# Hybrid gated-conv and forgetting-attention layer on one core: score buffers 192 bytes apart, later column sums, a residual added on TensorE, root and reciprocal in the final norm

## The chip, the cores and the metric

One Trainium2 chip, one core. The metric is the device time of the kernel in microseconds; three runs of the kernel before gave 702.77, 702.11 and 702.26 us, median 702.26 us. One further execution, of 702.7 us, was taken with the hardware profiler; its span (first to last instruction of the program) is 700.7 us. All rows of the profile and the trace are from that execution.

The engines go by short names: PE is TensorE (matmuls), PEld its loading of weights, DVE is VectorE, ACT is ScalarE, POOL is GpSimd, SP is SyncE (which only issues DMAs here). "L304" is line 304 of the kernel.

## The reference

One layer, 512 tokens of 1024 features, all in float32:

```
h = rms_norm(x) * g                       # over 1024 features
[cb|cc|cin|q|k|v|f|gates] = h @ w_in
y_conv = (cb * causal_dwconv3(cc * cin)) @ w_out_conv
F = cumsum(log_sigmoid(f))
o = softmax(q.k / 8 + F[t] - F[s], s <= t) v          # 8 heads of 64
m = sigmoid(g_A) * y_conv + sigmoid(g_B) * (o @ w_out_attn)
x = x + m @ w_o
h = rms_norm(x) * g_ffn
[a|b] = causal_dwconv3(h @ w_up)                      # 2 x 2816
x = x + (silu(a) * b) @ w_down
out = rms_norm(x) * g_final
```

`rms_norm(x)` is x / sqrt(mean(x^2) + 1e-6).

## The kernel before

**Data layout.** Features lie on the 128 partitions, in eight blocks of 128 (`KB`), tokens along the free axis (512). The residual stream is `x1`, called x in the trace. A matmul multiplies a weight tile of 128 x 128 by 256 tokens.

**Precision.** A float32 product is made of three matmuls on rounded halves: each operand is split into a high part (`h`) and the rest (`l`), and wh.xh, wl.xh and wh.xl are summed in PSUM (`mm3`, L286; `passes`, L304). The weights arrive raw in chunks, in the order of a list `stream`. For each chunk, `split` writes the high part with an ACT copy (L255, wh) and the rest with a DVE subtraction (L259, wl).

**Stages.** V projection; q and k projections with the attention scores between them; gates and the merge; w_o; the up projection with convolution and Silu (L1042), in two phases; the down projection, also in two phases, by a scheme of seven products for blocks of two by two (`seven`), with the additions collected in `combine`; at the end the last two feature blocks of the down projection as plain products (`plain7`, tiles pdA and pdB), and the final norm.

**Scores.** `scores` makes one 128-query tile of q.k for one head: a matmul of a_q (weights) with a_k (moving, L575), and a correction with qb (weights) and kb (moving, L576), into the same PSUM bank, 32 times in all. The moving width is 256, 384 or 512. These tiles come from a pool `ap`, which gives addresses in the order of allocation.

**Deferred work.** `later` holds small operations, each with the chunk number from which it is due, its estimated time and the PSUM banks that it frees. `run_later` pops due ones behind a split, `flush(banks)` pops from the front until no entry is left that touches those banks (all of them, without banks). The squares and the final scaling of the first six feature blocks (`final_square`) go through this list; the first two of them carry a due number, the others are due at once. On ACT a square is an activation from x (L1123, L1126), followed by a scaling of x (L1128), and on DVE an addition into ssq (L1127).

**The end.** `kall` is the list of the ten k-steps of a plain block. The tokens are in two halves: A (0 to 255) and B. The order on PE is written out by hand: both plain blocks of half A; five k-steps of the first block of half B (pdB6); the column sums of half A; the other five; the broadcast of half A's norm; the second block of half B (pdB7) in full; three filler matmuls (`warm_on`); the column sums of half B; six fillers; the broadcast of half B.

- `fin_sum` adds the residual (DVE, L1193), squares (ACT, L1195) and scales (ACT, L1196).
- `fin_col` adds one square into ssq (DVE, L1201) and calls `rstd_col`: the sums over the partitions (pc_n, L319, four passes for ssq and four for the last square), the mean plus eps (ms_n, DVE, L324) and the power -0.5 (rc_n, POOL, L326).
- `fin_out` broadcasts the result over the partitions with two matmuls (pb_n, L333), copies it for POOL (rs, ACT, L1208), multiplies (L1212) and sends the output.

Of the kernel before, what the change touches and what calls it, by code (L numbers as in the profile page):

```python
# [8 lines left out]
F32 = mybir.dt.float32  # L9
F32R = mybir.dt.float32r  # L10
AF = mybir.ActivationFunctionType
ALU = mybir.AluOpType

P = 128
D = 1024
S = 512
KB = D // P
NT = S // P
H = 8
# [3 lines left out]
NP = FFN // P  # L23
EPS = 1e-6
# [4 lines left out]
NPP = 4  # L29
# [5 lines left out]
G1, G2, GF, BG, CM, CF, BF = 0, 8, 16, 24, 40, 52, 184  # L35
# [31 lines left out]
def block_kernel(ctx, tc, xT, vecs, wv, win, wmix, wo, wup, wst, wdp, outT):  # L67
# [3 lines left out]
    nc = tc.nc  # L71
    PSUM = bass.MemoryType.PSUM

    cp = ctx.enter_context(tc.tile_pool(name="cp", bufs=1))
# [3 lines left out]
    def keep(ins):  # L78
        return tc.keep_in_program_order(ins)

    def bank(i, name):
        return ps.tile([P, S], F32, tag=f"b{i}", name=name)
# [14 lines left out]
    def col(i):  # L97
        return vec[:, i : i + 1]

    ident = cp.tile([P, P], F32, tag="ident", name="ident")  # L100
# [4 lines left out]
    tbl = cp.tile([4 * H, 1], F32, tag="tbl", name="tbl")  # L105
# [17 lines left out]
    n = 0  # L123
# [21 lines left out]
    raws, parts, order = [], [], {}  # L145
    pools = {"raw": wp}
    later = []
    held = dict.fromkeys(NRAW, 0)

    def after_split():  # L150

        st = ExitStack()
        for ins in order.values():
            st.enter_context(tc.issue_after(ins))
        return st
# [70 lines left out]

    def flush(banks=None):

        while any(banks is None or set(w[2]) & set(banks) for w in later):
            with after_split():  # L230
                later.pop(0)[3]()

    def split(hl=None):

# [72 lines left out]
            ))  # L307
            seen.add(bk)

    ex = cp.tile([P, NT], F32, tag="ex", name="ex")  # L310
    nc.gpsimd.memset(ex, -0.5)

    def rstd_col(sums, n, bc, name):


        pc = bank(bc, f"pc_{name}")
        for i, sq in enumerate(sums):
            for t in range(n):
                keep(nc.tensor.matmul(  # L319
                    pc[:, t : t + 1], sq[:, t * P : (t + 1) * P], ones[:, 0:1],  # L320
                    start=i == 0 and t == 0, stop=i == len(sums) - 1 and t == n - 1,
                ))
        ms = cp.tile([P, NT], F32, tag="ms", name=f"ms_{name}", bufs=2)
        nc.vector.tensor_scalar(ms[:, :n], pc[:, :n], 1.0 / D, EPS, op0=ALU.mult, op1=ALU.add)  # L324
        rc = cp.tile([P, NT], F32, tag="rc", name=f"rc_{name}", bufs=2)
        nc.gpsimd.tensor_tensor(rc[:, :n], ms[:, :n], ex[:, :n], op=ALU.pow)  # L326
        return rc
# [28 lines left out]
    ap = at.enter_context(tc.tile_pool(name="ap", bufs=1, side="right"))  # L356

    def ct(name):
        return ap.tile([P, S], F32, tag="ct", name=name, bufs=NCT)
# [15 lines left out]

    v2 = ap.tile([P, NT, 4, 2, 2, HD], F32R, tag="v2", name="v2")

    ssq = ct("ssq1")
    pa = [bank(t, f"pa{t}") for t in range(NT)]
    pb_ = [bank(4 + t, f"pb{t}") for t in range(NT // 2)]  # L380
# [3 lines left out]
    def load_x(kb, cs=slice(0, S)):  # L384
        if kb == len(xs):
            if kb % 2 == 0:
                load_x.t = ap.tile([P, 2, S], F32, tag="qt" if kb < 4 else "ka", name=f"xs{kb}", bufs=2)
            xs.append(load_x.t[:, kb % 2, :])
        keep(nc.sync.dma_start(xs[kb][:, cs], xT[:, kb, cs]))


    halves = [slice(0, S // 2), slice(S // 2, S)]
    load_x(0, halves[0])
    load(0)
    load_x(0, halves[1])
    for kb in range(1, AHEAD + 1):
        load_x(kb)
# [15 lines left out]
    for kb in range(KB):  # L413
        x = xs[kb]
# [70 lines left out]

    QB = [ap.tile([P, 2, S], F32R, tag=f"qb{i}", name=f"qb{i}") for i in range(2)]
    KBt = [ap.tile([P, 2, S], F32R, tag=f"kb{i}", name=f"kb{i}") for i in range(2)]
    AUX = (HD, 0)  # L490
    for t in (*QB, *KBt):
        tf = t.bitcast(F32)
# [8 lines left out]
    def evac_qk(pr, isq):  # L501
        def f(p):
# [6 lines left out]
            a = ap.tile([P, 2, S], F32R, tag="qt" if isq else "ka", name=f"a_{nm}", bufs=2)  # L509
            b = (QB if isq else KBt)[pr % 2]  # L510
            (QT if isq else KA)[pr] = a
# [58 lines left out]
    def scores(pr, e, qb):  # L570
# [5 lines left out]
        keep(nc.tensor.matmul(  # L576
            s[:, :nn], QB[pr % 2][: KR[e], e, qs], KBt[pr % 2][: KR[e], e, :nn], start=False, stop=True
        ))
# [72 lines left out]
    n = 4 * H  # L651
# [62 lines left out]
    for idx in late:  # L714
        kind, i = divmod(idx, 4)
# [7 lines left out]
    n = len(units)  # L723
    make_forms(0, len(GATES), "gate")
    for i in range(n + LA):
# [8 lines left out]
        if 0 <= i - LA < n:  # L734
            pr, e, qb = units[i - LA]
# [95 lines left out]
    def x_sums(qs):  # L831
        b11, b12, b21, b22 = (xq[:, qs, i, :] for i in range(4))

        def f():
            nc.vector.tensor_sub(b11, b11, b12)
            nc.vector.tensor_sub(b12, b22, b12)

        def g():
            nc.vector.scalar_tensor_tensor(b22, b11, -1.0, b22, op0=ALU.mult, op1=ALU.subtract)
            nc.vector.scalar_tensor_tensor(b21, b22, -1.0, b21, op0=ALU.mult, op1=ALU.subtract)  # L840

        return f, g
# [9 lines left out]
    for q in (0, 2):  # L852
        f, g = x_sums(slice(q, q + 2))
# [56 lines left out]
    for j in range(KB):  # L910
# [20 lines left out]
        a, b = gs  # L931
# [6 lines left out]
    x1 = xp.tile([P, KB, S], F32, tag="x1", name="x1")  # L938
# [70 lines left out]
    fp = ctx.enter_context(tc.tile_pool(name="fp", bufs=1))  # L1009
# [13 lines left out]
    def place(ph, q):  # L1023
        return (q - PHASES[ph][0] // 2) * (NF + ph)
# [13 lines left out]
    def glu(ph, j, uu):  # L1038
        a, b = uu
        q, k = j // 2, len(parts) - 1  # L1040
        g0 = place(ph, q)
        nc.scalar.activation(a, a, AF.Silu)  # L1042
        if j % 2 == 0:
            ge = glu.even = fp.tile([P, 2, 2 * P], F32, tag="ge", name=f"ge{q}", bufs=2)
            keep(nc.gpsimd.tensor_mul(ge, a.rearrange(halves_of, h=2), b.rearrange(halves_of, h=2)))  # L1045
            return
        flush()
        ge = glu.even
        go = fp.tile([P, 6, 2 * P], F32, tag="gr", name=f"go{q}")

        def mul(eng):
            return eng.tensor_mul(go[:, 0:2, :], a.rearrange(halves_of, h=2), b.rearrange(halves_of, h=2))

        if j + 1 < PHASES[ph][1]:
            keep(mul(nc.gpsimd))
        else:
            later.append((k + 3, 0.7, (("q", q),), lambda: mul(nc.vector)))
        b11, b12 = ge[:, 0, :], ge[:, 1, :]
        b21, b22, t1, t2, t3, t4 = (go[:, i, :] for i in range(6))

        def t13():
            nc.vector.tensor_sub(t1, b11, b12)
            nc.vector.tensor_sub(t3, b22, b12)

        def t24():
            nc.vector.scalar_tensor_tensor(t2, t1, -1.0, b22, op0=ALU.mult, op1=ALU.subtract)
            nc.vector.scalar_tensor_tensor(t4, t2, -1.0, b21, op0=ALU.mult, op1=ALU.subtract)

        def hl(src, gs):
            def f():  # L1070
                nc.scalar.activation(gh[:, gs, :], src, AF.Copy)
                nc.vector.tensor_sub(gl[:, gs, :], src, gh.bitcast(F32)[:, gs, :])

            return f


        d = (2, 3, 4) if j + 1 < PHASES[ph][1] else (4, 5, 6)
        w = [(d[0], 0.85, t13), (d[0], 0.85, t24), (d[1], 0.7, hl(ge[:, : 1 + ph, :], slice(g0, g0 + 1 + NF * ph, NF)))]
        w += [(d[x > 0 and 2 or 1], 0.7, hl(go[:, x : x + 2, :], slice(g0 + 1 + x, g0 + 3 + x))) for x in (0, 4, 2)]
        for n, us, f in w:  # L1080
            later.append((k + n, us, (("q", q),), f))
# [88 lines left out]
    kall = range(*PHASES[1])  # L1170

    def plain(m, t, ks, p, opens, closes):
        for k in ks:
            wh, wl = where[m, k]
            g = place(1, k // 2) + SLOT[k % 2][t]
            mm3(p, wh, wl, gh[:, g, :], gl[:, g, :], opens and k == kall[0], closes and k == kall[-1])

    m6 = KB - 2
# [6 lines left out]
    pd = ((pdA[:, th[0]], pdA[:, th[1]]), (pdB6[:, th[0]], pdB7[:, th[0]]))  # L1185

    def plain7(m, t, ks):
        plain(m6 + m, t, ks, pd[t][m], m == 0 or t == 1, m == 1 or t == 1)

    def fin_sum(t, m):  # L1190

        y = x1[:, m6 + m, halves[t]]
        nc.vector.tensor_add(y, pd[t][m], y)  # L1193
        sq = fp.tile([P, S], F32, tag="fu", name=f"sq3_{m}{t}", bufs=3)[:, : S // 2]
        nc.scalar.activation(sq, y, AF.Square)  # L1195
        nc.scalar.activation(y, y, AF.Copy, scale=col(GF + m6 + m))  # L1196
        return sq

    def fin_col(t, sqs):
        s_ = ssq3[:, halves[t]]  # L1200
        nc.vector.tensor_add(s_, s_, sqs[0])  # L1201
        return rstd_col([s_, sqs[1]], 2, 3 + t, f"n3{t}")

    def fin_out(t, rc):
        hs = halves[t]
# [15 lines left out]
    for m in range(2):  # L1221
        plain7(m, 0, kall)
    sqA = [fin_sum(0, 0), fin_sum(0, 1)]
    plain7(0, 1, kall[:5])
    rcA = fin_col(0, sqA)
    plain7(0, 1, kall[5:])
    fin_out(0, rcA)
    sqB = [fin_sum(1, 0)]
    plain7(1, 1, kall)
    sqB.append(fin_sum(1, 1))  # L1230
    warm_on(3)
    rcB = fin_col(1, sqB)
# [100 lines left out]
```

## Time and the profile before

| what | value |
|---|---|
| median of three runs | 702.26 us (702.11 to 702.77) |
| profiled execution | 702.7 us, span 700.7 us |
| granted TensorE clock, mean | 0.995 |
| busy: PE | 689.9 us of the span, 98% |
| busy: DVE, ACT, POOL | 72%, 49%, 25% |
| final stage, from the first matmul of pdB7 to the end of the span | 686.9 to 700.7 us |

How to read it: a row of the timeline gives start, duration, engine, line, operation, output and inputs, shape, the number of instructions in the row, and in brackets the idle time just before it with what ended it. A row of the waits gives who waited for whom: total, times, longest. A row of the chain gives start, duration, engine, tile, line; "issue" (not quoted) is time without a visible cause. A row of the groups gives total busy time and mean nanoseconds of one, then idle time before. Matmuls overlap in the pipeline, so their rate is the distance from start to start and not the duration of one.

### The profile page before, as it was taken

Reading aid. Unit: us, or ns where it says so; the run is one execution under the profiler, and the core shown is the slowest. Engines: PE = TensorE matmul, PEld = TensorE weight load, DVE = VectorE, ACT = ScalarE, POOL = GpSimd, SP = SyncE. Lnnn points to the kernel's source line nnn. Section 1 sums busy time; section 2 is a strip of 40 time slices with the busy share of each in tenths; the row PEclk is TensorE's granted clock in tenths of the full one; section 3 lists DMA queues with packets and bytes.
Section 4 is the critical chain, followed back from the end, with each engine's and each line's share of the span. In section 5 each row is a group of like instructions: output and inputs, shape, how many; then the busy total and the mean of one; then the engine's idle time right before and its main releaser. Section 6 shows DMA issues by size and latency. Waiting matters only on the chain. (4 is left out here: it accounts for less than half of the span.)

```text
span 700.7 us, 14594 instructions
## 1 busy us (share of the span) xinstructions
PE 689.9 (98%) x6006; PEld 687.9 (98%) x6006; DVE 501.8 (72%) x783; ACT 341.7 (49%) x540; POOL 173.0 (25%) x188
## 2 busy tenths in 40 slices
PE   8999999999999999999999999999999999999995
PEld 8999999999999999999999999999999999999995
DVE  6678877776677778754377777777774677877783
ACT  5564655645565444443345543455443345444562
POOL 4124847532200000224413214100000322311002
PEclk9999999999999999999999999999999999999998
DMA  7527978542442555687977756545546785676403
GB/s 252 159 80 253 206 192 204 116 93 86 159 163 89 176 190 173 191 292 147 228 187 167 207 121 136 165 144 186 186 146 206 152 203 138 182 199 166 142 22 121
DMA packets 52578, 116.02 MB, mean 166 GB/s; under 512 B 4848, under 2 KB 23296, under 8 KB 52512
## 3 DMA queue, kind: packets, MB, share of 16 engines
q1 hardware_dynamic: 37456, 94.16, 40.7%
q0 software_dynamic: 13792, 19.72, 17.4%
q10 hardware_dynamic: 1264, 1.22, 0.5%
q8 instruction: 47, 0.77, 0.4%
q14 instruction: 19, 0.16, 0.1%
HBM read 112.92 MB, written 33.03 MB: 208 GB/s over the span
## 5 line engine op out<-in xcount | busy, mean ns | idle before, releaser
L286 PE MATMUL p_up<-x1h,wh_up 128*128 128x256 f32 x536 | 104.5, 276 | 0.0
L286 PE MATMUL p_up<-x1h,wl_up 128*128 128x256 f32 x536 | 104.4, 276 | 0.0
L286 PE MATMUL p_up<-x1l,wh_up 128*128 128x256 f32 x536 | 104.3, 276 | 0.0
L255 ACT ACTIVATE wh_up<-raw_up 128x1024 fp32r<-128x1024 f32 x44 | 46.7, 1060 | 89.1 <-PE p_up L286 68.8
L286 PEld LDWEIGHTS p_up<-x1h,wl_up 128*128 128x128 f32 x536 | 80.8, 188 | 0.0
L286 PEld LDWEIGHTS p_up<-x1h,wh_up 128*128 128x128 f32 x536 | 80.7, 188 | 0.0
L286 PEld LDWEIGHTS p_up<-x1l,wh_up 128*128 128x128 f32 x536 | 80.6, 188 | 0.0
L259 DVE TENSOR_TENSOR wl_up<-raw_up,wh_up 128x1024 fp32r<-128x1024 f32 x44 | 53.8, 1223 | 20.6 <-ACT wh_up L255 20.6
L1045 POOL TENSOR_TENSOR ge<-fu,fu 128x512 f32<-128x512 f32 x11 | 17.1, 1552 | 161.7 <-DVE fu L533 142.8
L286 PE MATMUL p_in<-xgh,wh_in 128*128 128x256 f32 x288 | 56.8, 279 | 0.0
L286 PE MATMUL p_in<-xgh,wl_in 128*128 128x256 f32 x288 | 56.6, 278 | 0.2 <-DVE wl_in L259 0.2
L286 PE MATMUL p_in<-xgl,wh_in 128*128 128x256 f32 x288 | 56.5, 277 | 0.0
L201 POOL DMA_DIRECT2D f<-in_wst_dram x48 | 55.8, 1282 | 0.0
L1032 DVE TENSOR_TENSOR fz<-p_up,rb_n 128x512 f32<-128x512 f32 x44 | 30.3, 690 | 31.6 <-PE p_up L286 31.5
L259 DVE TENSOR_TENSOR wl_F<-raw_F,wh_F 128x1024 fp32r<-128x1024 f32 (+1 forms) x30 | 40.4, 1346 | 14.3 <-ACT wh_F L255 14.3
L255 ACT ACTIVATE wh_F<-raw_F 128x1024 fp32r<-128x1024 f32 (+1 forms) x30 | 31.6, 1052 | 30.3 <-PE dn L304 25.8
L286 PEld LDWEIGHTS p_in<-xgh,wh_in 128*128 128x128 f32 x288 | 44.7, 188 | 0.7
L286 PEld LDWEIGHTS p_in<-xgh,wl_in 128*128 128x128 f32 x288 | 43.5, 188 | 0.4 <-DVE wl_in L259 0.4
L286 PEld LDWEIGHTS p_in<-xgl,wh_in 128*128 128x128 f32 x288 | 43.6, 188 | 0.0
L304 PE MATMUL p_up<-x1h,wh_up 128*128 128x256 f32 x168 | 40.3, 277 | 0.0
L304 PE MATMUL p_up<-x1l,wh_up 128*128 128x256 f32 x168 | 40.2, 276 | 0.0
L259 DVE TENSOR_TENSOR wl_in<-raw_in,wh_in 128x1024 fp32r<-128x1024 f32 x26 | 34.6, 1332 | 7.3 <-ACT wh_in L255 7.1
(306 smaller groups left out, 2033.8 us busy)
## 6 DMA issues: line engine op xcount, KB each, us to landing
raw_up<-in_wup_dram SPq DMA_DIRECT2D x44, 512.0 KB, 4.8
raw_F<-f SPq DMA_DIRECT2D x29, 512.0 KB, 4.3
raw_in<-in_win_dram SPq DMA_DIRECT2D x26, 512.0 KB, 3.6
raw_P<-in_wst_dram SPq DMA_DIRECT2D x29, 384.0 KB, 3.7
f<-in_wst_dram POOLq DMA_DIRECT2D x29, 256.0 KB, 5.6
f<-in_wst_dram SPq DMA_DIRECT2D x14, 512.0 KB, 6.1
f<-in_wst_dram POOLq DMA_DIRECT2D x14, 512.0 KB, 7.9
f<-f SPq DMA_DIRECT2D x28, 256.0 KB, 5.2
```

The source lines that it names most:

```text
L201: return lambda: keep(nc.gpsimd.dma_start(dst, src, accum_op=ALU.add))
L255: ins = nc.scalar.activation(hi, raw, AF.Copy)
L259: ins = nc.vector.tensor_sub(lo, raw, hi.bitcast(F32))
L286: keep(nc.tensor.matmul(out[:, cs], w, x[:, cs], start=start and i == 0 and c == 0, stop=stop and i == 2 and c == len(cut) - 1,))
L304: keep(nc.tensor.matmul(out, wl if x == 1 else wh, xl if x == 2 else xh, start=opens and bk not in seen, stop=closes and bk not in left,))
L1032: nc.vector.tensor_mul(z, p, rb2)
L1045: keep(nc.gpsimd.tensor_mul(ge, a.rearrange(halves_of, h=2), b.rearrange(halves_of, h=2)))
```

## The change

Five edits.

1. `flush` with banks no longer takes everything from the front of `later`: it takes the first entry that is wanted (touches the banks) or is due by its chunk number.
2. `qb` and `kb` are allocated earlier in the pool `ap`, and one tile each of `pp` and `m` is allocated before the last input tiles. Only addresses follow from this: the distance from a_q to a_k goes from 8192 bytes to 16576 bytes a partition, which is 192 more than a multiple of 512, and the distance from qb to a_k also gets an offset of 192.
3. The column sums of half A come after seven k-steps of pdB6 and not after five.
4. The residual of the last block of half B is added on PE: its values are split into high and low part (yhl, by ACT and DVE), and two matmuls with an identity matrix in the rounded format (`identr`, written by ACT) add them into pdB7 after its fourth k-step. `fin_sum` then squares and scales directly from PSUM.
5. In both halves of the final norm the mean and the power become one ACT square root (scale 1/1024, bias eps) and one DVE reciprocal. Sqrt needs another activation table; a small activation (`tbl`) behind the last Silu brings it in.

```diff
@@ -226,9 +226,13 @@
 
     def flush(banks=None):
 
-        while any(banks is None or set(w[2]) & set(banks) for w in later):
+        def wanted(w):
+            return set(w[2]) & set(banks) if banks is not None else True
+
+        while any(map(wanted, later)):
+            n = next(n for n, w in enumerate(later) if banks is None or wanted(w) or w[0] < len(parts))
             with after_split():
-                later.pop(0)[3]()
+                later.pop(n)[3]()
 
     def split(hl=None):
 
@@ -307,10 +311,12 @@
             ))
             seen.add(bk)
 
-    ex = cp.tile([P, NT], F32, tag="ex", name="ex")
-    nc.gpsimd.memset(ex, -0.5)
-
-    def rstd_col(sums, n, bc, name):
+    ex = cp.tile([P, 2 * NT], F32, tag="ex", name="ex")
+    nc.gpsimd.memset(ex[:, :NT], -0.5)
+    nc.gpsimd.memset(ex[:, NT:], EPS)
+    eps = ex[:, NT : NT + 1]
+
+    def rstd_col(sums, n, bc, name, root=False):
 
 
         pc = bank(bc, f"pc_{name}")
@@ -321,6 +327,11 @@
                     start=i == 0 and t == 0, stop=i == len(sums) - 1 and t == n - 1,
                 ))
         ms = cp.tile([P, NT], F32, tag="ms", name=f"ms_{name}", bufs=2)
+        if root:
+            nc.scalar.activation(ms[:, :n], pc[:, :n], AF.Sqrt, scale=1.0 / D, bias=eps)
+            rc = cp.tile([P, NT], F32, tag="rc", name=f"rc_{name}", bufs=2)
+            nc.vector.reciprocal(rc[:, :n], ms[:, :n])
+            return rc
         nc.vector.tensor_scalar(ms[:, :n], pc[:, :n], 1.0 / D, EPS, op0=ALU.mult, op1=ALU.add)
         rc = cp.tile([P, NT], F32, tag="rc", name=f"rc_{name}", bufs=2)
         nc.gpsimd.tensor_tensor(rc[:, :n], ms[:, :n], ex[:, :n], op=ALU.pow)
@@ -375,6 +386,8 @@
 
     v2 = ap.tile([P, NT, 4, 2, 2, HD], F32R, tag="v2", name="v2")
 
+    QB = [ap.tile([P, 2, S], F32R, tag=f"qb{i}", name=f"qb{i}") for i in range(2)]
+    KBt = [ap.tile([P, 2, S], F32R, tag=f"kb{i}", name=f"kb{i}") for i in range(2)]
     ssq = ct("ssq1")
     pa = [bank(t, f"pa{t}") for t in range(NT)]
     pb_ = [bank(4 + t, f"pb{t}") for t in range(NT // 2)]
@@ -384,6 +397,9 @@
     def load_x(kb, cs=slice(0, S)):
         if kb == len(xs):
             if kb % 2 == 0:
+                if kb == 4:
+                    ap.tile([P, S], F32, tag="pp", name="pp_", bufs=NPP)
+                    ap.tile([P, 4], F32, tag="m", name="m_", bufs=6)
                 load_x.t = ap.tile([P, 2, S], F32, tag="qt" if kb < 4 else "ka", name=f"xs{kb}", bufs=2)
             xs.append(load_x.t[:, kb % 2, :])
         keep(nc.sync.dma_start(xs[kb][:, cs], xT[:, kb, cs]))
@@ -485,8 +501,6 @@
 
 
 
-    QB = [ap.tile([P, 2, S], F32R, tag=f"qb{i}", name=f"qb{i}") for i in range(2)]
-    KBt = [ap.tile([P, 2, S], F32R, tag=f"kb{i}", name=f"kb{i}") for i in range(2)]
     AUX = (HD, 0)
     for t in (*QB, *KBt):
         tf = t.bitcast(F32)
@@ -1040,6 +1054,8 @@
         q, k = j // 2, len(parts) - 1
         g0 = place(ph, q)
         nc.scalar.activation(a, a, AF.Silu)
+        if j == NP - 1:
+            nc.scalar.activation(tbl, a[: 4 * H, :1], AF.Sqrt, scale=0.0, bias=eps[: 4 * H])
         if j % 2 == 0:
             ge = glu.even = fp.tile([P, 2, 2 * P], F32, tag="ge", name=f"ge{q}", bufs=2)
             keep(nc.gpsimd.tensor_mul(ge, a.rearrange(halves_of, h=2), b.rearrange(halves_of, h=2)))
@@ -1187,9 +1203,21 @@
     def plain7(m, t, ks):
         plain(m6 + m, t, ks, pd[t][m], m == 0 or t == 1, m == 1 or t == 1)
 
+    identr = fp.tile([P, P], F32R, tag="identr", name="identr")
+    nc.scalar.activation(identr, ident, AF.Copy)
+    y_last = x1[:, KB - 1, halves[1]]
+    yhl = fp.tile([P, 2, 2 * P], F32R, tag="fz", name="yhl", bufs=2)
+    nc.scalar.activation(yhl[:, 0, :], y_last, AF.Copy)
+    nc.vector.tensor_sub(yhl[:, 1, :], y_last, yhl.bitcast(F32)[:, 0, :])
+
     def fin_sum(t, m):
 
         y = x1[:, m6 + m, halves[t]]
+        if t == m == 1:
+            sq = fp.tile([P, S], F32, tag="fu", name=f"sq3_{m}{t}", bufs=3)[:, : S // 2]
+            nc.scalar.activation(sq, pd[t][m], AF.Square)
+            nc.scalar.activation(y, pd[t][m], AF.Copy, scale=col(GF + m6 + m))
+            return sq
         nc.vector.tensor_add(y, pd[t][m], y)
         sq = fp.tile([P, S], F32, tag="fu", name=f"sq3_{m}{t}", bufs=3)[:, : S // 2]
         nc.scalar.activation(sq, y, AF.Square)
@@ -1199,7 +1227,7 @@
     def fin_col(t, sqs):
         s_ = ssq3[:, halves[t]]
         nc.vector.tensor_add(s_, s_, sqs[0])
-        return rstd_col([s_, sqs[1]], 2, 3 + t, f"n3{t}")
+        return rstd_col([s_, sqs[1]], 2, 3 + t, f"n3{t}", root=True)
 
     def fin_out(t, rc):
         hs = halves[t]
@@ -1221,12 +1249,15 @@
     for m in range(2):
         plain7(m, 0, kall)
     sqA = [fin_sum(0, 0), fin_sum(0, 1)]
-    plain7(0, 1, kall[:5])
+    plain7(0, 1, kall[:7])
     rcA = fin_col(0, sqA)
-    plain7(0, 1, kall[5:])
+    plain7(0, 1, kall[7:])
     fin_out(0, rcA)
     sqB = [fin_sum(1, 0)]
-    plain7(1, 1, kall)
+    plain7(1, 1, kall[:4])
+    for x in range(2):
+        keep(nc.tensor.matmul(pd[1][1], identr, yhl[:, x, :], start=False, stop=False))
+    plain7(1, 1, kall[4:])
     sqB.append(fin_sum(1, 1))
     warm_on(3)
     rcB = fin_col(1, sqB)
```

How the rows of each engine stand now. A row names line, operation, output, inputs and width; the numbers behind the names count the buffers.

PE around the column sums of half A: pdB6 is the first plain block of half B, ones is the column of ones that sums over the partitions. Before:

```order
L286 MATMUL pdB6_8618<-gl_4480,wh_dp0_8578 128x256
L319 MATMUL pc_n30_8705<-ones_71,ssq3_4481 128x1 x2
L319 MATMUL pc_n30_8705<-ones_71,sq3_10_8686 128x1 x2
L286 MATMUL pdB6_8618<-gh_4479,wh_dp0_8578 128x256
L286 MATMUL pdB6_8618<-gh_4479,wl_dp0_8579 128x256
```

And now, from the same place:

```order
L290 MATMUL pdB6_8622<-gl_4483,wh_dp0_8582 128x256
L290 MATMUL pdB6_8622<-gh_4482,wh_dp0_8582 128x256
L290 MATMUL pdB6_8622<-gh_4482,wl_dp0_8583 128x256
L290 MATMUL pdB6_8622<-gl_4483,wh_dp0_8582 128x256
L290 MATMUL pdB6_8622<-gh_4482,wh_dp0_8582 128x256
L290 MATMUL pdB6_8622<-gh_4482,wl_dp0_8583 128x256
L290 MATMUL pdB6_8622<-gl_4483,wh_dp0_8582 128x256
L325 MATMUL pc_n30_8720<-ones_71,ssq3_4484 128x1 x2
L325 MATMUL pc_n30_8720<-ones_71,sq3_10_8695 128x1 x2
```

Two k-steps, six matmuls, have moved from behind the sums to ahead of them.

ACT in the final stage, from the squares of the last two combined blocks to the copy of half A's broadcast (rs). Before:

```order
L1126 ACTIVATE sq_2_8609<-x_3957 128x512
L1126 ACTIVATE sq_3_8613<-x_3957 128x512
L1128 ACTIVATE x_3957<-x_3957,vec 128x512 x2
L1195 ACTIVATE sq_00_8682<-x_3957 128x256
L1195 ACTIVATE sq_10_8686<-x_3957 128x256
L1196 ACTIVATE x_3957<-x_3957,vec 128x256 x2
L1208 ACTIVATE rs_8732<-pb_n_8729 128x256
```

And now:

```order
L1142 ACTIVATE sq_2_8613<-x_3960 128x512
L1210 ACTIVATE yhl<-x_3960 128x256
L1144 ACTIVATE x_3960<-x_3960,vec 128x512
L1142 ACTIVATE sq_3_8617<-x_3960 128x512
L1223 ACTIVATE sq_00_8691<-x_3960 128x256
L1144 ACTIVATE x_3960<-x_3960,vec 128x512
L1224 ACTIVATE x_3960<-x_3960,vec 128x256
L1223 ACTIVATE sq_10_8695<-x_3960 128x256
L1224 ACTIVATE x_3960<-x_3960,vec 128x256
L331 ACTIVATE ms_n_8725<-pc_n_8720,ex 128x2
L1236 ACTIVATE rs_8741<-pb_n_8738 128x256
```

The split of the residual (yhl) and one scaling stand ahead of the second square, a scaling ahead of the last one, and the square root (ms_n) ahead of rs.

ACT around the first two deferred squares (ssq and sq_5), between two weight splits. Before:

```order
L255 ACTIVATE wh_P_8462<-raw_P_8273 128x768
L1123 ACTIVATE ssq_4481<-x_3957 128x512
L1126 ACTIVATE sq_5_8468<-x_3957 128x512
L1128 ACTIVATE x_3957<-x_3957,vec 128x512 x2
L255 ACTIVATE wh_F_8492<-raw_F_8305 128x1024
```

And now:

```order
L259 ACTIVATE wh_P_8466<-raw_P_8277 128x768
L1139 ACTIVATE ssq_4484<-x_3960 128x512
L1142 ACTIVATE sq_5_8472<-x_3960 128x512
L1144 ACTIVATE x_3960<-x_3960,vec 128x512 x2
L259 ACTIVATE wh_F_8496<-raw_F_8309 128x1024
```

Here no row has moved.

## The prediction

> **What bounds the kernel now.** The page of the profile comes first: one engine is busy for nearly the whole span, so only what TensorE (PE) issues, or what it waits for, can change the time.
>
> ```profile
> span 700.7 us, 14594 instructions
> PE 689.9 (98%) x6006; PEld 687.9 (98%) x6006; DVE 501.8 (72%) x783; ACT 341.7 (49%) x540; POOL 173.0 (25%) x188
> ```
>
> Next, the waits of PE. These four are the ones that the change comes near.
>
> ```profile
> PE dn L304 <- ACT wh_F L255: 0.9, 1, 0.9
> PE pc_n L319 <- DVE ssq L1201: 0.5, 1, 0.5
> PE pc_n L319 <- ACT sq L1195: 0.3, 1, 0.3
> PE pb_n L333 <- POOL rc_n L326: 0.2, 1, 0.2
> ```
>
> They are small, each happens once, and three of them lie in the final norm. Behind the last product the kernel has no PE work to hide anything, so there the chain of waits counts in full:
>
> ```profile
> 687.14 3.46 PE pdB L286 x30
> 690.62 0.44 DVE x L1193
> 691.08 0.42 ACT sq L1195
> 691.55 0.62 PE pc_n L319 x4
> 692.19 0.17 DVE ms_n L324
> 692.43 0.71 POOL rc_n L326
> 693.18 0.72 PE pb_n L333 x4
> 693.99 0.39 ACT rs L1208
> ```
>
> Read downwards: residual add, square, column sums, mean, power -0.5, broadcast, copy. The change touches the first, second, fourth and fifth link. The profiled execution took 702.7 us, 2.0 more than its span; the median of the three runs is 702.26 (702.11 to 702.77). I sum changes against the profiled execution and carry the difference to the median. 0.2%, about what a measurement of this kernel can tell from no change, is 1.4 us.
>
> **The deferred squares.** The rule of flush is rewritten, but around the squares the order of instructions on ACT and PE is the same in both kernels; only line and buffer numbers differ. So the wait of 0.9 us for wh_F stays, with its cause:
>
> ```profile
> 663.71 0.62 ACT L1123 ACTIVATE ssq<-x 128x512 f32<-128x512 f32 x1
> 665.98 1.04 ACT L255 ACTIVATE wh_F<-raw_F 128x1024 fp32r<-128x1024 f32 x1
> ```
>
> The squares and scalings still stand ahead of this weight split on ACT. Term: 0.
>
> **The column sums of half A.** They stand after five of ten products of one block, and PE stops in front of them:
>
> ```profile
> 683.05 0.28 PE L286 MATMUL pdB<-gl,wh_dp 128*128 128x256 f32 x1
> 683.85 0.58 PE L319 MATMUL pc_n<-ones,ssq 128*128 128x1 f32 x4 [0.52 <-DVE ssq L1201]
> 684.29 0.58 PE L319 MATMUL pc_n<-ones,sq 128*128 128x1 f32 x4
> ```
>
> From start to start that is 0.80 us, where a product matmul takes 0.115 (30 in 3.46, chain): 0.69 is lost. Now six matmuls (0.69) come first, so PE reaches the sums at 683.05 + 0.115 + 0.69 = 683.85, just when they were ready before. But the operand comes later, since a copy (ACT) and a subtraction (DVE) for the new residual are slipped in ahead:
>
> ```profile
> 680.98 1.49 DVE L1127 TENSOR_TENSOR ssq<-ssq,sq 128x512 f32<-128x512 f32 x2
> 682.38 0.75 DVE L1193 TENSOR_TENSOR x<-pdA,x 128x256 f32<-128x256 f32 x2
> 683.28 0.42 DVE L1201 TENSOR_TENSOR ssq<-ssq,sq 128x256 f32<-128x256 f32 x1 [0.15 <-ACT sq L1195]
> ```
>
> DVE now does one sum into ssq (0.70), the subtraction (0.35), two adds (0.35 each), the second sum (0.70), then L1201 (0.42): from 680.98 to some 683.85. The sums start 0.15 later (683.70 to 683.85 before), at 684.0. About 0.17 is still lost, so the term is -0.5; ends 0.2 (the copy delays ACT's squares by another 0.3) and 0.69 (no wait left). Root and reciprocal of half A end at about 685.6 (sums 1.0, two short instructions); PE, having lost less, reaches the broadcast near 686.0 and waits for nothing.
>
> **Two matmuls for the last residual.** identr times the high and the low part of y_last, both 256 columns wide like the products: 2 x 0.115 = +0.23, in full on the path.
>
> Their weight, identr, is written by ACT long before, between two splits, and this is the wait that the change adds: for the eight loads of xr and for POOL's last ssq add of the second norm.
>
> ```profile
> 341.80 1.79 POOL L952 TENSOR_TENSOR ssq<-ssq,sq 128x512 f32<-128x512 f32 x1 [2.67 <-ACT sq L951]
> 348.53 1.06 ACT L255 ACTIVATE wh_up<-raw_up 128x1024 fp32r<-128x1024 f32 x1 [6.87 <-issue]
> ```
>
> The add ends at 343.6, the copy takes about 0.3; queued behind it is the split of wh_up at 348.53, with 6.9 us of idle ACT ahead. The cover is over 4 us. Term: 0.
>
> **The tail of half B.** With E = 690.58, the end of the last product matmul, before: broadcast at 693.18 = E + 2.60.
>
> ```profile
> 690.30 0.28 PE L286 MATMUL pdB<-gl,wh_dp 128*128 128x256 f32 x1
> 690.42 0.52 PE L1218 MATMUL warm_to<-gl,gh 128*128 128x256 f32 x3
> 690.78 0.50 PE L319 MATMUL pc_n<-ones,ssq 128*128 128x1 f32 x4
> 692.01 0.96 PE L1218 MATMUL warm_to<-gl,gh 128*128 128x256 f32 x6
> ```
>
> After: Square reads PSUM itself and ends near E + 0.46; what is late next is PE, whose three fillers and first sums hold it to 690.78 + 0.45 = E + 0.65. The second sums take 0.58 without a wait (row at 684.29): E + 1.23. Root over two columns: between this short activation
>
> ```profile
> 2.02 0.20 ACT L106 ACTIVATE tbl<-ones 32x1 f32<-32x1 f32 x1
> ```
>
> and the 0.39 of rs with 256 columns; I take 0.26, near the short one. The reciprocal costs what the mean cost on DVE, 0.17. With 0.03 at each hand-over: E + 1.75. The six fillers begin at E + 1.10 and take 0.69, so the broadcast starts at about E + 1.8 either way. Saved: 2.60 - 1.80 = 0.8, ends 0.6 (root 0.39, slow hand-overs) and 0.9. Hidden in it are the add (0.46), the mean and the power (0.98 with hand-overs) against root and reciprocal (0.5).
>
> **The root's table.** A table load and a short activation now stand behind the last Silu.
>
> ```profile
> 357.07 1.28 ACT L1042 ACT_TABLE_LOAD   x1 [1.57 <-DVE fu L533]
> 358.36 0.63 ACT L1042 ACTIVATE fu<-fu 128x512 f32<-128x512 f32 x1
> 635.77 0.63 ACT L1042 ACTIVATE fu<-fu 128x512 f32<-128x512 f32 x1 [1.92 <-DVE fu L533]
> 637.83 1.06 ACT L255 ACTIVATE wh_F<-raw_F 128x1024 fp32r<-128x1024 f32 x1 [1.43 <-PE p_up L286]
> 639.67 0.28 PE L304 MATMUL dn<-gh,wh_F 128*128 128x256 f32 x1
> ```
>
> A load takes 1.28, and the next activation starts 0.01 after it. 635.77 + 0.63 + 1.28 + 0.20 = 637.88, against 637.83 where the split behind it starts; its result is needed at 639.67, 0.8 after its end. Term: 0.
>
> The Trainium skill ("ScalarE: Activation LUTs", What ACT_TABLE_LOAD costs) adds a drain of about 1.38 us to each load, which would make the switch some 2.66. The rows at 357.07 and 358.36 show no drain behind the load; if there were one, the sum would be 0.65 worse, which is a rival below.
>
> **The score buffers.** Only addresses move. What the order of operands in memory costs, the trace shows only in this place: one score product, then its correction, same width.
>
> ```profile
> 134.44 0.38 PE L604 MATMUL tp<-ident,pp 128*128 128x128 f32 x2
> 134.57 0.48 PE L575 MATMUL s<-a_k,a_q 128*128 128x512 f32 x1
> 134.89 0.39 PE L576 MATMUL s<-kb,qb 128*128 128x512 f32 x1
> 135.12 0.40 PE L286 MATMUL p_in<-xgh,wh_in 128*128 128x256 f32 x2
> L575 PE MATMUL s<-a_k,a_q 128*128 128x256 f32 x16 | 5.4, 337 | 0.0
> L576 PE MATMUL s<-kb,qb 128*128 128x256 f32 x8 | 2.2, 280 | 0.0
> ```
>
> The correction takes 0.23 to the next start. Transposes and product together take 0.45; two transposes at a broadcast's pace (0.72 for four, so 0.18) and 0.23 leave 0.03 as a possible conflict at the widest; a third less on average, over 32 pairs 0.6. If the transposes account for it all, it is 0. By the row means it is 57 ns x 32 = 1.8, but those durations overlap their neighbours. I take -0.4, between the first two, and keep 0 and 1.1 (0.03 x 32, rounded up) as ends.
>
> **Sum.** -0.5 + 0.23 - 0.8 - 0.4 = -1.47: 702.7 becomes 701.2, and the median 702.26 becomes 700.8. With all ends together: from -0.69 + 0.23 - 0.9 - 1.1 = -2.5 (699.8) to -0.2 + 0.23 - 0.6 = -0.6 (701.7).
>
> **The rivals.**
>
> *The addresses bring nothing and the sums still stop PE.* For it: the pair of 512 columns can be explained without a conflict, and L1201 does come later. Then -0.2 + 0.23 - 0.8 = -0.8: 701.5. Chance 0.08.
>
> *The table switch is longer.* If the switch lasted 1.38 more, wh_F would end at 640.3 and PE would wait 0.65: 701.4. Against it speaks the row at 358.36. Chance 0.05.
>
> *Something gains in full.* Either the address conflict is what the row means say (1.8 for 0.4), or the squares leave their place after all (0.9 more), that is, the order doesn't tell what the chip does: 699.4 to 699.9. Chance 0.06.
>
> *identr holds up the splits (slower).* If one of its waits ended late, the splits of wh_up would queue behind it. ACT has until 348.2; PE follows some 2 us later, and from there each microsecond costs one. To end slower than 703.66 the wait must eat the gain of 1.47 and 1.4 more, so must end after about 353; 354 would give 704.4. Against it: the loads belong to sums that end at 343.6. Chance 0.05, with 0.03 more for a new conflict at the tiles that moved along with the score buffers.
>
> **How the numbers follow.** The forecast, 700.8, has 0.73. It straddles 700.86, the edge of 0.2%; its address term reaches further down than up, so 0.48 of it is faster and 0.25 the same. With the rivals: faster 0.54, same 0.38 (0.25 + 0.08 + 0.05), slower 0.08. The range of 699.7 to 701.9 takes in the ends of all terms and the two rivals within 0.2%.
>
> **What would show it.** In the profile after: the wait for L1201 down to under 0.3; the wait for wh_F at 667 unchanged; no wait of PE at 639.7 nor near 352; from the last product matmul to the broadcast 1.8 us; no POOL power in the last 20 us. The attention stage, from its first score to its last, should be shorter by up to 1 us with the same instructions. If that stage gains over 1 us, or if PE waits in a new place, the prediction is wrong there.

## The result, and the profile after

Measured side by side in 22 runs each, the changed kernel takes 701.52 us (median), the kernel before 702.31: a ratio of 0.9989 with a 95% interval of 0.9982 to 0.9995. The gain is 0.79 us or 0.11%, real but within the 0.2% of "same". The forecast was 700.8. The profiled execution took 702.08 us with a span of 700.0.

Two lines of the page and one of the waits of PE, of the kernel after:

```profile
span 700.0 us, 14606 instructions
PE 690.9 (99%) x6008; PEld 689.2 (98%) x6008; DVE 501.7 (72%) x783; ACT 344.0 (49%) x546; POOL 171.5 (24%) x187
PE dn L308 <- ACT wh_F L259: 0.9, 1, 0.9
```

All three waits of the final norm have left the list. The one for wh_F, behind the deferred squares, is there as before. The chain of waits at the end, of the kernel after:

```profile
688.41 0.23 PE pdB L1259 x2
688.65 2.06 PE pdB L290 x18
690.70 0.36 PE warm_to L1246 x3
691.06 0.79 PE pc_n L325 x8
691.85 0.81 PE warm_to L1246 x6
692.66 0.46 PE pb_n L344 x4
```

Before, this part of the chain went through DVE, ACT and POOL. Now it is PE alone up to the broadcast: the products, three fillers, the sums and six fillers decide when it starts, and root and reciprocal end before PE needs them. The two residual matmuls are the first row.

The timeline of PE shows the two places that moved (column sums of half A; last product and broadcast of half B):

```profile
684.19 0.28 PE L290 MATMUL pdB<-gl,wh_dp 128*128 128x256 f32 x1
684.40 0.58 PE L325 MATMUL pc_n<-ones,ssq 128*128 128x1 f32 x4
690.43 0.28 PE L290 MATMUL pdB<-gl,wh_dp 128*128 128x256 f32 x1
692.50 0.61 PE L344 MATMUL pb_n<-ident,rc_n 128*128 128x128 f32 x4
```

Product to column sums is 0.21 us, not 0.80. From E = 690.71, the end of the last product, to the broadcast it is 1.79 us, not 2.60. From the timeline of DVE and ACT around them:

```profile
683.83 0.43 DVE L1229 TENSOR_TENSOR ssq<-ssq,sq 128x256 f32<-128x256 f32 x1
691.88 0.26 ACT L331 ACTIVATE ms_n<-pc_n,ex 128x2 f32<-128x2 f32 x1 [0.40 <-PE pc_n L325]
692.17 0.17 DVE L333 RECIPROCAL rc_n<-ms_n 128x2 f32<-128x2 f32 x1 [2.41 <-ACT ms_n L331]
```

The addition into ssq for which the column sums wait (L1229) ends at 684.26, so PE still loses 0.10 us in front of them. Root 0.26 and reciprocal 0.17 are as predicted; the broadcast would have its operand at 692.34, and PE comes at 692.50.

The last Silu, the table load and identr, from the timeline of ACT, and the first product that needs the split behind the load, from that of PE:

```profile
636.02 0.64 ACT L1056 ACTIVATE fu<-fu 128x512 f32<-128x512 f32 x1 [1.92 <-DVE fu L547]
636.68 1.28 ACT L1058 ACT_TABLE_LOAD   x1
637.97 0.29 ACT L1058 ACTIVATE tbl<-fu,ex 32x1 f32<-32x1 f32 x1
638.17 1.04 ACT L259 ACTIVATE wh_F<-raw_F 128x1024 fp32r<-128x1024 f32 x1
639.93 0.28 PE L308 MATMUL dn<-gh,wh_F 128*128 128x256 f32 x1
343.88 0.31 ACT L1207 ACTIVATE identr<-ident 128x128 fp32r<-128x128 f32 x1 [1.97 <-POOL ssq L966]
348.74 1.06 ACT L259 ACTIVATE wh_up<-raw_up 128x1024 fp32r<-128x1024 f32 x1 [4.55 <-PE p_up L290]
```

Neither costs PE anything. The split behind the load ends at 639.21, 0.7 us before PE needs it, and 4.55 us of idle ACT are left behind identr.

So three terms came out as summed. What the sum missed is in the attention stage. The same two matmuls, the third score product and the first product behind the stage, in the timeline of PE of before and then of after:

```profile
59.44 0.28 PE L575 MATMUL s<-a_k,a_q 128*128 128x256 f32 x1
182.75 0.45 PE L286 MATMUL yc<-ych,wh_mix 128*128 128x256 f32 x2
```

```profile
59.42 0.28 PE L589 MATMUL s<-a_k,a_q 128*128 128x256 f32 x1
183.00 0.45 PE L290 MATMUL yc<-ych,wh_mix 128*128 128x256 f32 x2
```

123.31 us before, 123.58 after: the new addresses were to gain 0.4 us and seem to lose 0.27.

### The profile page after: what moved, and what is told of

The parts are those of the page before. It is cut to its first block, busy times and chain, and to the rows that moved or that the text cites. A ratio compares the mean times of both kernels' runs of the same rounds, so it can differ in the third digit from the quotient of the medians.

```text
span 700.0 us, 14606 instructions
## 1 busy us (share of the span) xinstructions
PE 690.9 (99%) x6008; PEld 689.2 (98%) x6008; DVE 501.7 (72%) x783; ACT 344.0 (49%) x546; POOL 171.5 (24%) x187
## 5 line engine op out<-in xcount | busy, mean ns | idle before, releaser
L263 DVE TENSOR_TENSOR wl_up<-raw_up,wh_up 128x1024 fp32r<-128x1024 f32 x44 | 53.8, 1223 | 20.6 <-ACT wh_up L259 20.6
```

Source lines behind the costliest of these rows:

```text
L263: ins = nc.vector.tensor_sub(lo, raw, hi.bitcast(F32))
```

## The experiments

The theory: every part is worth its own term on PE's path, and the addresses cost some 0.25 us. Rivals: that delay is chance; the table switch or the residual split hands back what the tail gains. Stretches of one trace are read as the distance between the starts of the same two matmuls, since the first 9 us of an execution differ by themselves (last section). The stretch for the addresses starts behind PE's last wait in the attention stage, near 53.8 us, whose end also differs by some hundredths of a microsecond from trace to trace.

**The addresses alone.** Only the allocations of qb, kb and the two extra tiles are taken over.

> The kernel before with the new addresses of the score buffers and nothing else. Theory (the addresses are worse by a little): PE reaches the first matmul of the gates stage about 0.25 us later than in the trace of before, as it does after the change; time 702.5. Rival (that delay is chance of one execution): the delay is under 0.1 us; time 702.3. The prediction's term, 0.4 us gained: 701.9. The stretch at 667 to 672 us keeps its pace of 0.113 us a matmul if its slowing after the change comes from another part.

Measured: 702.98 us, ratio 1.0003 (0.9994 to 1.0012), which decides nothing. The trace does (timeline of PE of this kernel):

```profile
58.89 0.28 PE L578 MATMUL s<-a_k,a_q 128*128 128x256 f32 x1
182.47 0.45 PE L286 MATMUL yc<-ych,wh_mix 128*128 128x256 f32 x2
```

123.58 us, 0.27 more than before and the same as after the whole change. The loss goes with the addresses.

**The kernel before, once more.** No edit.

> The kernel before, profiled once more, to see what one execution differs from the next in. If the delays of 0.25 us in the attention stage and of 0.20 us at 667 to 672 us come from the change, this trace lies on the first one within 0.05 us at every matmul up to 683 us; if they are chance, it drifts by as much.

One run, 702.45 us. Its timeline of PE:

```profile
58.85 0.28 PE L575 MATMUL s<-a_k,a_q 128*128 128x256 f32 x1
182.16 0.45 PE L286 MATMUL yc<-ych,wh_mix 128*128 128x256 f32 x2
```

The two matmuls start 123.31 us apart, exactly as in the first trace of before; chance is out as a cause in the attention stage. The other traces of this section say the same: this stretch takes 123.31 us in all eight with the old addresses or with the earlier allocation alone, and 123.58 in all four with the whole address edit. At 667 us chance is not out, as these rows show: the first product behind the wait for wh_F and the first of the plain blocks, in before and in before once more:

```profile
667.07 0.39 PE L304 MATMUL dn<-gh,wh_F 128*128 128x256 f32 x1 [0.88 <-ACT wh_F L255]
674.66 0.28 PE L286 MATMUL pdA<-gh,wh_dp 128*128 128x256 f32 x1
```

```profile
666.56 0.39 PE L304 MATMUL dn<-gh,wh_F 128*128 128x256 f32 x1 [0.83 <-ACT wh_F L255]
674.34 0.28 PE L286 MATMUL pdA<-gh,wh_dp 128*128 128x256 f32 x1
```

7.59 and 7.78 us: this stretch has two paces, in the same kernel. After the change it takes 7.78 (667.35 to 675.13). The 0.19 us by which that trace is behind here need not be an effect of the change; what sets the pace is not known.

**The changed kernel with the old addresses.** The hunks on qb, kb, pp_ and m_ are undone.

> The changed kernel with the old addresses. Theory (the addresses cost 0.25 us): 701.3, and PE comes to the gates stage as early as in the trace of before. Rival (the addresses are worth nothing): 701.5, the same as the changed kernel. By the prediction's term it would be 0.4 us slower, 701.9.

Measured: 701.11 us, ratio to before 0.9981 (0.9972 to 0.9990), against 0.9989 for the full change. The intervals overlap, so the medians agree with a loss of 0.3 us without showing it; the stretch, 123.31 us, shows it.

**Which part of the address edit.** One kernel takes only the earlier allocation, one only the extra tiles, one adds 64 bytes to the full edit.

```diff
 # addr_q: before, with this alone
+    QB = [ap.tile([P, 2, S], F32R, tag=f"qb{i}", name=f"qb{i}") for i in range(2)]   # ahead of ssq1
+    KBt = [ap.tile([P, 2, S], F32R, tag=f"kb{i}", name=f"kb{i}") for i in range(2)]
 # addr_pp: before, with this alone
+                if kb == 4:
+                    ap.tile([P, S], F32, tag="pp", name="pp_", bufs=NPP)
+                    ap.tile([P, 4], F32, tag="m", name="m_", bufs=6)
 # addr_256: the full address edit, and this behind m_
+                    ap.tile([P, 16], F32, tag="gap", name="gap_")
```

> The kernel before with qb and kb allocated earlier, without the two tiles that make the 192 bytes: all score buffers trade places, but every distance among them stays a multiple of 512 bytes. If the 192 bytes make the loss, PE's drift against the trace of before between 50 and 183 us is under 0.05 us; if the new places do, it is 0.27.

> The kernel before with the two tiles and without the earlier allocation: a_k gets its 192 bytes against a_q, and qb and kb move along by the same 192, so that they stand to a_k as before. If the offset of a_k against a_q makes the loss, the drift is 0.27 us as with the whole edit; if that against qb makes it, under 0.05.

> The kernel with the new addresses, and 64 bytes more between the buffers: the offset is 256 bytes and not 192 (what lies before them moves by 64). If 192 is only a bad number, the drift between 50 and 183 us falls under 0.1 us or turns into a gain; if any offset costs the same, it stays near 0.27.

Measured, in one run each (702.81, 702.26 and 702.64 us). The timelines of PE, first of the earlier allocation, then of the extra tiles:

```profile
59.43 0.28 PE L575 MATMUL s<-a_k,a_q 128*128 128x256 f32 x1
182.73 0.45 PE L286 MATMUL yc<-ych,wh_mix 128*128 128x256 f32 x2
```

```profile
58.81 0.28 PE L578 MATMUL s<-a_k,a_q 128*128 128x256 f32 x1
182.18 0.45 PE L286 MATMUL yc<-ych,wh_mix 128*128 128x256 f32 x2
```

The earlier allocation costs nothing (123.30 by these rows, within 0.01 of before). The extra tiles cost 0.06 us (123.37), both together 0.27, and with 256 bytes it is 0.34 (58.87 to 182.52), so no better. Among the score tiles, what only the kernels with the large loss have is an offset of a_k against qb and kb; in the second half those move along with a_k. The offset of a_k against a_q, which that half has, goes with the 0.06. Other tiles of the pool moved as well, so the pair of tiles is narrowed down and not proved.

The time is not lost in the score products, though. From start to start, summed over the traces of before and after, only 0.05 of the 0.27 us comes up at the 30 pairs of product and correction in this stretch. 0.22 comes up between the projection matmuls (p_in) that stand between them, a few nanoseconds at a time. As an example, one run of 24 projection matmuls, from the first one to the transposes behind the last, before and then after:

```profile
83.51 0.39 PE L286 MATMUL p_in<-xgh,wh_in 128*128 128x256 f32 x2
86.24 0.60 PE L604 MATMUL tp<-ident,pp 128*128 128x128 f32 x4
```

```profile
83.57 0.40 PE L290 MATMUL p_in<-xgh,wh_in 128*128 128x256 f32 x2
86.34 0.60 PE L618 MATMUL tp<-ident,pp 128*128 128x128 f32 x4
```

2.73 us before, 2.77 after. The projections read xgh, xgl and the weights, which lie in other pools and did not move. Why they are slower is open.

**The parts at the end, one at a time**, each on the kernel before. First the column sums:

```diff
-    plain7(0, 1, kall[:5])
+    plain7(0, 1, kall[:7])
     rcA = fin_col(0, sqA)
-    plain7(0, 1, kall[5:])
+    plain7(0, 1, kall[7:])
```

> The kernel before with the column sums of half A after seven k-steps and not five. Theory (a wait shortened by 0.59 us): the distance from the last product to the sums falls from 0.80 to 0.11 us, as no residual split delays DVE here; 0.69 gained, time 701.6. Rival (half of the gain is handed back at the broadcast of half A, whose root of the mean goes through POOL and comes later): a wait of 0.3 us in front of that broadcast; time 701.9.

Measured: 701.87 us, ratio 0.9989 (0.9981 to 0.9998). Product to sums is 0.12 us (683.32 to 683.44), so 0.68 is gained there. At the broadcast of half A 0.15 is handed back: from the product ahead of it to the one behind it, it is 0.62 us (685.36 to 685.98), where it was 0.47 (686.42 to 686.89). POOL's power ends at 685.46 and the broadcast starts at 685.51, so the rival's cause is there, at less than half of its size. Alone, this edit gives as large a gain, by the medians, as the whole change.

Then root and reciprocal (with their table load), and the residual on TensorE:

> The kernel before with the square root and the reciprocal in the last norms, and with the table load behind the last Silu. Theory: the tail from the last product matmul to the broadcast falls from 2.60 to 2.13 us, bound by the six fillers; PE does not wait at 639.7; time 701.85. Rival (the table switch holds up the split behind it): PE waits 0.3 us or more near 640.

> The kernel before with the last residual added by two matmuls and squared from PSUM, sums and power as before. Theory: 0.23 us for the two matmuls; in return the second column sums follow the first without a gap and start 0.32 us earlier after the last product; the split of the residual delays the sums of half A, still after five k-steps, by 0.5 us; time 702.7, slower alone. Rival (the residual matmuls are free): 702.2 or less.

Measured: root 702.3 us, ratio 0.9996 (0.9987 to 1.0005); residual 702.46, ratio 0.9999 (0.9991 to 1.0008); neither can be told from no change by its time. In their timelines of PE, last product and broadcast, first for root, then for the residual:

```profile
690.44 0.28 PE L286 MATMUL pdB<-gl,wh_dp 128*128 128x256 f32 x1
692.95 0.61 PE L340 MATMUL pb_n<-ident,rc_n 128*128 128x128 f32 x4
```

```profile
690.18 0.28 PE L286 MATMUL pdB<-gl,wh_dp 128*128 128x256 f32 x1
692.63 0.71 PE L333 MATMUL pb_n<-ident,rc_n 128*128 128x128 f32 x4 [0.21 <-POOL rc_n L326]
```

From the end of the product (start + 0.28) to the broadcast: 2.23 and 2.17 us, so 0.37 and 0.43 less than 2.60, together 0.80 of the 0.81 of the whole change. Root alone was expected at 2.13: the six fillers and the turn to the broadcast take 0.80 (692.15 to 692.95), not 0.69. The residual alone pays 0.23 for its matmuls; its split delays the sums of half A by 0.09 only (0.89 us behind the product at 682.55), where 0.5 was expected.

**The squares really moved.** On top of the change, the first two deferred squares become due one chunk later:

```diff
-            first = [c[0] for c in stream].index(f"F{len(DOUBLES) - 2}") if i == 0 else 0
+            first = [c[0] for c in stream].index(f"F{len(DOUBLES) - 2}") if i != 1 else 0
             for m in (2 * i, 2 * i + 1):
-                later.append((first, 0.8, (), lambda m=m: final_square(m)))
+                later.append((first, 0.4 if i == 2 else 0.8, (), lambda m=m: final_square(m)))
```

> The changed kernel with the first two deferred squares really behind the next weight split: they become due one chunk later, with a smaller estimated time, so that both fit there. Theory: the wait of 0.88 us for that split at 667 us goes, and nothing comes in its place; 700.6. Rival (the squares come late for the column sums of half A, or the combine step ahead of the split waits for PE): part of the gain returns as a wait at 684 us or at 667 us; 701.2.

Measured: 701.17 us, ratio 0.9980 (0.9971 to 0.9988). ACT, PE and DVE in the timeline of this kernel, and its waits of PE:

```profile
663.75 1.05 ACT L259 ACTIVATE wh_F<-raw_F 128x1024 fp32r<-128x1024 f32 x1
664.70 0.62 ACT L1139 ACTIVATE ssq<-x 128x512 f32<-128x512 f32 x1
665.13 0.84 PE L308 MATMUL dn<-gh,wl_P 128*128 128x256 f32 x6
665.81 0.28 PE L308 MATMUL dn<-gh,wh_F 128*128 128x256 f32 x1
682.48 0.43 DVE L1229 TENSOR_TENSOR ssq<-ssq,sq 128x256 f32<-128x256 f32 x1 [0.15 <-ACT sq L1223]
PE pc_n L325 <- DVE ssq L1229: 0.4, 1, 0.4
```

The split is now ahead of the squares, and PE goes straight on at 665.81: 0.68 us from row to row, where it was 1.72 after the change (665.63 to 667.35). But of what the column sums of half A wait for, not everything comes as much earlier. From the trace after to this one, the last product ahead of them starts 1.83 us earlier (684.19 to 682.36), and their operand ends only 1.35 earlier (684.26 to 682.91). The wait there is back with 0.4 us (682.36 to 683.05 from product to sums, 0.69 and not 0.21). The rival was right: of 1.04 us gained, 0.48 is handed back at 683 us.

**All of it tuned together.** On top of that, column sums after eight k-steps, two and five fillers; then the same with the old addresses.

> The same with the column sums of half A after eight k-steps, two fillers and not three ahead of the last column sums, five and not six behind them. Theory: 0.10 from the sums, 0.11 and 0.12 from the fillers, which ended last in front of the second sums and of the broadcast; 0.3 below the kernel with the squares moved, 700.3. Rival (root and reciprocal end last then): the broadcast starts only 0.1 us earlier; 700.45.

> The best kernel so far (squares moved, column sums after eight k-steps, two and five fillers) with the old addresses of the score buffers. Theory (the addresses cost 0.27 us of PE's time, the same in every execution): 0.27 below it, 700.1. Rival (the addresses are worth nothing in the whole): 700.4.

Measured: 700.38 us, ratio 0.9967 (0.9954 to 0.9980), and 700.38 us, 0.9965 (0.9952 to 0.9979). Both beat the two given kernels. The old addresses show in the trace (123.31 us for the stretch of the attention stage, against 123.58) and not in the time: 700.1 had been expected for them, and five runs each do not tell 0.27 us apart. In the timeline of PE of the first of them:

```profile
688.89 0.28 PE L290 MATMUL pdB<-gl,wh_dp 128*128 128x256 f32 x1
690.79 0.71 PE L344 MATMUL pb_n<-ident,rc_n 128*128 128x128 f32 x4
```

End of product to broadcast is 1.62 us, 0.17 less than with three and six fillers, between theory (0.23) and rival (0.1); now the reciprocal ends last (690.75) in front of the broadcast. The column sums of half A start 0.37 us behind their product, not 0.69.

## Why the prediction was right or wrong

The range held the time, and the direction was right. The size was not: 0.79 us for 1.47, and the likelier side of 0.2%, at 0.54, was the wrong one. That the range held is owed to the terms of the final norm; the address term had the wrong sign, and the width of the range covered it. Term by term:

| term | predicted | traces |
|---|---|---|
| column sums of half A | -0.5 | -0.59 (0.80 to 0.21) |
| two residual matmuls | +0.23 | +0.23 |
| tail of half B | -0.8 | -0.81 (2.60 to 1.79) |
| score buffers | -0.4 | +0.27, alone +0.27 |
| squares, table load, identr | 0 | 0 |
| sum | -1.47 | -0.90 |

With the slower pace at 667 us (0.19) the sum gives -0.71; the spans of the two traces, 700.7 and 700.0, differ by 0.7. So the terms account for the pair of traces.

The step that failed is the score buffers. It read a conflict into 0.03 us that could not be assigned to the transposes, and let the row means of the two score products (337 and 280 ns) push the value up. Its working has a slip: 0.72 for four is 0.18 for one, so two transposes would take 0.36, more than was there to share out. By the starts of the broadcast's row and the row behind it, 686.53 and 686.89 in the timeline of before, four take 0.36; that gives the 0.18, and then 0.04 and not 0.03 is left. Nor was this the only place to look. The first four score products stand behind projections and not behind transposes. One of them, with its correction and the matmul behind, in the timeline of PE of before:

```profile
56.45 0.28 PE L575 MATMUL s<-a_k,a_q 128*128 128x256 f32 x1
56.57 0.28 PE L576 MATMUL s<-kb,qb 128*128 128x256 f32 x1
56.68 0.40 PE L286 MATMUL p_in<-xgh,wh_in 128*128 128x256 f32 x2
```

Product and correction take 0.12 and 0.11 us, the pace of the products elsewhere: at 256 columns the old addresses show no conflict. At the pair of 512 columns that the working used, product to correction takes about 0.32 us from start to start in both traces, and the mean of that product goes from 476 to 479 ns: the new addresses removed nothing there either. The low end, put at 0 for this term, should have gone below it, since an address edit moves other pairs of tiles too; the text had that only as a chance of 0.03 beside a rival.

The rival at 701.5, addresses without effect and sums still stopping PE, hit the time by luck, with another mix: the addresses cost, and the sums wait less than it said.

The rest of the working stood. PE's hold on the tail was named (fillers until E + 1.8; measured 1.79), and so was the later operand of the column sums: 0.17 was to be lost (0.15 by its own times, 684.0 less 683.85), 0.10 was. The term of 0 for the rewritten flush held, since the rows had not moved, and the wait of 0.88 stayed.

The table switch went as the rows had said: the load starts 0.02 us behind the Silu, the next activation 0.01 behind the load, at 637.97, and PE did not wait. The Trainium skill ("ScalarE: Activation LUTs", What ACT_TABLE_LOAD costs) adds a drain of about 1.38 us to a load. No such drain shows in this trace.

## What to carry to other kernels

On an engine that is 98% busy, look for the few waits that are left and price each from start to start; here those terms were forecast to 0.1 us. Then ask of each wait removed which operand comes next: the squares moved behind their split gave 1 us at 667 and lost half of it at 683. An effect of addresses that no row shows should be given both signs, and before it is priced, look for the same instruction in another neighbourhood: here the first score products had no transposes ahead of them and showed no conflict.

## What had not been expected of the hardware

- The placement of buffers changes the pace of PE by a fixed amount: 123.31 us for one stretch of the attention stage in every trace with the old addresses, 123.58 in the four with the whole address edit, and most of the difference comes up at matmuls whose own operands did not move.
- A stretch of 66 matmuls near the end takes 7.59 or 7.78 us in the same kernel.
- Two executions of the same kernel reach the third score product 0.59 us apart (59.44 and 58.85 us), from waits in the first 9 us, one of them 0.84 us long in the one and 0.29 in the other. That alone is three quarters of the effect that was to be measured, which is why stretches of the trace decide here where medians cannot.
